# An expert layer's first panels as 512-column products, their two sums added by chains, and a shorter routing

## The chip, the cores and the metric

The kernel runs on one core of one Trainium2 chip. The metric is the time of one execution on the device in microseconds. A row of the profile gives start times from the first instruction of the profiled execution.

## The reference

Two transformer blocks run one behind the other on 256 tokens of width 1024; all is float32. The change lies in `peer`, a layer of 16384 experts that the second block has in each of its two layers (layer 0 and layer 1):

```python
def peer(xn, wq, k1, k2, u_tab, v_tab):
    q = (xt @ wq).reshape(t, PEER_HEADS, D_KEY)          # 8 heads, 2 halves of 128
    s1 = jnp.einsum("thd,hnd->thn", q1, k1)              # 128 keys a half
    s2 = jnp.einsum("thd,hnd->thn", q2, k2)
    v1, i1 = lax.top_k(s1, TOPK)                         # 16 best of each half
    v2, i2 = lax.top_k(s2, TOPK)
    cand = (v1[..., :, None] + v2[..., None, :]).reshape(t, PEER_HEADS, TOPK * TOPK)
    sv, ci = lax.top_k(cand, TOPK)                       # 16 best of the 256 pairs
    e1 = jnp.take_along_axis(i1, ci // TOPK, axis=-1)
    e2 = jnp.take_along_axis(i2, ci % TOPK, axis=-1)
    gates = jax.nn.softmax(sv, axis=-1)
    ...
        hid = jax.nn.gelu(jnp.einsum("td,tkd->tk", xi, u_tab[ei]))
        return jnp.einsum("tk,tkd->td", gi * hid, v_tab[ei])
```

## The kernel before

Every float32 weight panel of 128x1024 is loaded by SyncE (`raw`), copied to a rounded part `whi` by ScalarE (ACT), and the rest `wlo = raw - whi` is made by VectorE (DVE). The tokens stand as two such parts too, `xh` and `xl`, side by side in one tile `xhl`. A product is then three: hi times xh, lo times xh, hi times xl. TensorE (PE) does them at its fast float32 rate. `raw` has four buffers, `whi` and `wlo` three each; `ahead` makes the parts of the panel two further on while a panel is multiplied.

An expert layer does not gather experts: it multiplies all tokens by all of `u` (128 panels of 128 experts), gates the result, and multiplies it by all of `v` (128 panels). It has these stages, here with layer 0's times:

- `wq` (from 1049.0 us): 16 panels make the queries, `scores` the scores, and `firsts` takes the 16 best of each half with `top16` on VectorE: max of eight, their indices, replace, and again.
- `u` (1101.5 to 1529.9 us): 128 panels through `feat`, which does 24 products of 256 columns each: 8 by hi on xh, 8 by lo on xh, 8 by hi on xl. Two panels share one PSUM bank of the pair `w`, and `late` then applies gelu on ACT and multiplies by the gate on DVE.
- beside it on DVE, in this order: what is left of `firsts`, `route(0)` and `route(1)` (the 256 pairs, their 16 best, and the two look-ups by comparing with 0 to 15), and `builds`: for four tokens at a time `onehots` (four `oha` and two `ohb` on DVE, the other two `ohb` on ACT), `gates` (products of these on PE into a PSUM bank, which say how much gate each expert of each token has), and `place`, which moves a bank of gates into `G` and `H`: experts not yet reached are copied by ACT, those already done are multiplied by DVE.
- `v` (from 1531.1 us): 128 panels through `krow`.

The order on each engine is fixed before the run by a planner. `Clock` estimates each instruction, and `Chains` holds the side work as generators. `chains.run()`, called between products, steps a generator when the estimated time of PE has reached its due time: the estimated end of its last step plus 0.2 us less the lead that it yielded (`LEAD_TOP` 1.0, `LEAD_BUILD` 0.8, else 0). `chains.idle()` steps one whether due or not. PSUM has eight banks: two `w`, two `b`, four `acc`. `gates` goes round the four `acc` banks.

The line of nearly all instructions in the trace is that of the helper that records them, L226.

Of the kernel before, what the change touches and what calls it, by code (L numbers as in the profile page):

```python
# [9 lines left out]
F32 = mybir.dt.float32  # L10
# [3 lines left out]
AF = mybir.ActivationFunctionType  # L14
# [274 lines left out]
def net(tc, A, out, stop=None):  # L289
# [3 lines left out]
    with ctx:  # L293
# [86 lines left out]

        banks = [0]

        def feat_sum(dst, other):


            banks[0] += 1
            ps = bank() if banks[0] & 2 else other()
# [10 lines left out]
            chains.run()  # L398
            nc.scalar.activation(dst, ps[:, T:], AF.Copy)
            nc.vector.tensor_tensor(dst, dst, ps[:, :T], op=OP.add)  # L400

        def nat(ps, xh, xl):

# [879 lines left out]
        def peer(l, acc, soon):  # L1283
            with tc.tile_pool(name=f"peer{l}", bufs=1) as p:
# [77 lines left out]
                def route(c):  # L1362
                    r = R[c]
                    v, i, fi, cf, ef, sv, ci, cs, cand = (r[n] for n in ("v", "i", "fi", "cf", "ef", "sv", "ci", "cs", "cand"))
                    nc.vector.tensor_copy(fi, i)
                    for b in (slice(0, 4), slice(4, 8)):
                        nc.vector.tensor_tensor(cand[:, b], v[:, 0, b][:, :, :, None].to_broadcast([128, 4, 16, 16]),
                                                v[:, 1, b][:, :, None, :].to_broadcast([128, 4, 16, 16]), op=OP.add)
                        yield
                    for h in range(8):  # L1370
                        yield from top16(sv[:, h], ci[:, h], cand[:, h].rearrange("p a b -> p (a b)"))
                        yield LEAD_TOP
                    nc.vector.tensor_scalar(cs, ci, 4, None, op0=OP.logical_shift_right)
                    nc.vector.tensor_copy(cf[:, 0], cs)
                    nc.vector.tensor_scalar(cs, ci, 15, None, op0=OP.bitwise_and)
                    nc.vector.tensor_copy(cf[:, 1], cs)
                    yield
                    for s in range(2):
                        for b in (slice(0, 4), slice(4, 8)):
                            nc.vector.tensor_tensor(cand[:, b], cf[:, s, b][:, :, :, None].to_broadcast([128, 4, 16, 16]),  # L1380
                                                    iota[:, None, None, 0:16].to_broadcast([128, 4, 16, 16]),
                                                    op=OP.is_equal)
                            yield
                            nc.vector.tensor_tensor(cand[:, b], cand[:, b],
                                                    fi[:, s, b][:, :, None, :].to_broadcast([128, 4, 16, 16]), op=OP.mult)
                            yield
                            nc.vector.tensor_reduce(ef[:, s, b], cand[:, b], axis=AX.X, op=OP.add)
                            yield
# [20 lines left out]
                state = {"u": 0, "t": 0}  # L1409

                def onehots(t0):
                    a = p.tile([128, 4, 128], F32, name="oha", bufs=2)
# [11 lines left out]

                def gates(t0, a, b):

                    i = t0 // 4 % 4
                    ps = psum.tile([128, 512], F32, name=f"acc{i // 2}{i % 2}", bufs=1)
                    for j in range(4):
                        mm(ps[:, j * 128:(j + 1) * 128], a[:, j], b[:, j], start=True, stop=True)  # L1430
                    return ps
# [23 lines left out]
                        yield LEAD_BUILD  # L1455
                    place(*last)

                def late(e, ps):

                    nt, g = state["t"], rows(e, 2)  # L1460
                    pv = ps.rearrange("p (a t) -> p a t", a=2)
# [237 lines left out]
```

## Time and profile before

| what | before |
|---|---|
| median of 3 runs | 2845.87 us (2844.71 to 2847.70) |
| the profiled execution | 2847.0 us, span 2845.2 us |
| TensorE busy | 2794.8 us, 98% |
| VectorE busy | 2045.7 us, 72% |
| ScalarE busy | 1494.0 us, 53% |
| `u` stage, layer 0 | 1101.5 to 1529.9 us |
| `u` stage, layer 1 | 2060.1 to 2488.4 us |

Durations of neighbours on VectorE and on TensorE overlap in the trace, since an instruction's end is written back while the next one works. What an instruction costs its queue is therefore the distance of two starts, not its duration.

### The profile page before, as it was taken

Reading aid. Unit: us, or ns where it says so; the run is one execution under the profiler, and the core shown is the slowest. Engines: PE = TensorE matmul, PEld = TensorE weight load, DVE = VectorE, ACT = ScalarE, POOL = GpSimd, SP = SyncE. Lnnn points to the kernel's source line nnn. Section 1 sums busy time; section 2 is a strip of 40 time slices with the busy share of each in tenths; the row PEclk is TensorE's granted clock in tenths of the full one; section 3 lists DMA queues with packets and bytes.
Section 4 is the critical chain, followed back from the end, with each engine's and each line's share of the span. In section 5 each row is a group of like instructions: output and inputs, shape, how many; then the busy total and the mean of one; then the engine's idle time right before and its main releaser. Section 6 shows DMA issues by size and latency. Waiting matters only on the chain.

```text
span 2845.2 us, 47840 instructions
## 1 busy us (share of the span) xinstructions
PE 2794.8 (98%) x18786; PEld 2553.3 (90%) x18786; DVE 2045.7 (72%) x3710; ACT 1494.0 (53%) x2423; POOL 100.7 (4%) x104
## 2 busy tenths in 40 slices
PE   9999999999999999999999999999999999999999
PEld 9988889998887889999998888887999999988887
DVE  5556665666766889988995555569898899755555
ACT  4444545544454654447764444456444677544444
POOL 1001010000101100000000000010000000000000
PEclk9999999999999999999999999999999999999999
DMA  6445556544554344554345555543455433455554
GB/s 242 163 164 179 187 176 199 172 148 138 187 192 156 127 144 161 193 181 138 127 138 181 194 195 194 202 159 122 162 180 190 165 127 134 159 190 193 193 194 161
DMA packets 135969, 484.18 MB, mean 170 GB/s; under 512 B 17152, under 2 KB 18176, under 8 KB 135744
## 3 DMA queue, kind: packets, MB, share of 16 engines
q1 hardware_dynamic: 132064, 468.07, 48.2%
q0 software_dynamic: 3680, 13.05, 1.4%
q8 instruction: 148, 2.42, 0.3%
q14 instruction: 77, 0.63, 0.1%
HBM read 479.92 MB, written 1.15 MB: 169 GB/s over the span
## 4 chain that ended last, share of the span: by engine, by line
PE 51%; issue 13%; DVE 2%; ACT 1%; POOL 0%; DVEq 0%; POOLq 0%; ACTq 0%
PE w L226 30%; PE acc L226 19%; DVE G L226 2%; PE b L226 1%; ACT G L226 0%; ACT whi L226 0%; DVE wlo L226 0%; DVE xN L226 0%; ACT ohb L226 0%; POOL r L226 0%; POOL wlo L226 0%; ACT xhl L226 0%; POOL G L226 0%; ACT w L226 0%; DVE nm L226 0%
## 5 line engine op out<-in xcount | busy, mean ns | idle before, releaser
L226 DVE TENSOR_TENSOR wlo<-raw,whi 128x1024 fp32r<-128x1024 f32 (+1 forms) x874 | 1062.6, 1219 | 551.8 <-ACT whi L226 546.1
L226 ACT ACTIVATE whi<-raw 128x1024 fp32r<-128x1024 f32 (+1 forms) x881 | 924.4, 1053 | 673.5 <-PE acc L226 386.4
L226 PE MATMUL w<-xhl,whi 128*128 128x256 f32 (+1 forms) x6176 | 869.5, 292 | 4.4 <-ACT whi L226 4.2
L226 PEld LDWEIGHTS w<-xhl,whi 128*128 128x128 f32 x6176 | 795.4, 193 | 20.8 <-ACT whi L226 5.0
L226 PE MATMUL acc<-whi,xhl 128*128 128x512 f32 x2048 | 550.2, 390 | 2.4 <-ACT xhl L226 2.4
L226 PE MATMUL w<-xhl,wlo 128*128 128x256 f32 x3248 | 462.4, 286 | 9.4 <-DVE wlo L226 9.3
L226 PEld LDWEIGHTS acc<-whi,xhl 128*128 128x128 f32 x2048 | 384.5, 188 | 82.3 <-ACT xhl L226 2.8
L226 PEld LDWEIGHTS w<-xhl,wlo 128*128 128x128 f32 x3248 | 422.5, 193 | 15.4 <-DVE wlo L226 11.2
L226 PE MATMUL acc<-wlo,xhl 128*128 128x512 f32 x1024 | 317.7, 389 | 0.0
L226 PEld LDWEIGHTS acc<-wlo,xhl 128*128 128x128 f32 x1024 | 192.3, 188 | 39.8
L226 ACT ACTIVATE G<-w 128x512 f32<-128x512 f32 (+16 forms) x157 | 81.6, 520 | 203.1 <-PE w L226 202.6
L226 DVE TENSOR_SCALAR oha<-iota,e1T,gT 128x128 f32<-128x128 f32 x512 | 152.8, 341 | 0.0
L226 PE MATMUL acc<-ohb,oha 128*128 128x128 f32 x1024 | 136.7, 276 | 0.3
L226 PEld LDWEIGHTS acc<-ohb,oha 128*128 128x128 f32 x1024 | 125.9, 192 | 2.0 <-ACT ohb L226 1.4
L226 PE MATMUL w<-whi,xhl 128*128 128x256 f32 x640 | 121.2, 287 | 0.0
L226 PEld LDWEIGHTS w<-whi,xhl 128*128 128x128 f32 x640 | 101.9, 193 | 2.3 <-issue 2.1
L226 PE MATMUL w<-wlo,xhl 128*128 128x256 f32 x320 | 91.3, 285 | 0.3
L226 POOL TENSOR_TENSOR r<-v,minus_half 128x1 f32<-128x1 f32 x26 | 21.8, 840 | 1959.5 <-DVE v L226 1959.5
L226 ACT ACTIVATE ohb<-iota,me2T 128x128 f32<-128x128 f32 x256 | 87.5, 392 | 0.7 <-PE acc L226 0.7
L226 PE MATMUL b<-xhl,whi 128*128 128x512 f32 x320 | 80.2, 393 | 0.0
L226 DVE TENSOR_TENSOR xhl<-G,xhl 128x512 fp32r<-128x512 f32 x112 | 76.5, 684 | 0.0
L226 DVE TENSOR_TENSOR G<-G,acc 128x272 f32<-128x272 f32 (+22 forms) x128 | 66.5, 520 | 8.5 <-ACT H L226 8.2
(303 smaller groups left out, 2962.1 us busy)
## 6 DMA issues: line engine op xcount, KB each, us to landing
raw<-u SPq DMA_DIRECT2D x256, 512.0 KB, 3.2
raw<-v SPq DMA_DIRECT2D x256, 512.0 KB, 3.3
raw<-ffn SPq DMA_DIRECT2D x132, 512.0 KB, 4.0
raw<-mix SPq DMA_DIRECT2D x90, 512.0 KB, 3.3
raw<-att SPq DMA_DIRECT2D x80, 512.0 KB, 3.3
raw<-ret SPq DMA_DIRECT2D x63, 512.0 KB, 3.3
bias<-scr POOLq DMA_DIRECT2D x12, 512.0 KB, 7.1
G<-norm_g SPq DMA_DIRECT2D x4, 512.0 KB, 5.6
```

The lines of the kernel that those rows point to most:

```text
L226: return f(*args, **kw)
```

## The change

`feat_both` does a `u` panel as `feat_sum` did elsewhere already: 8 products by hi on both parts of the tokens (512 columns), 8 by lo on xh (256 columns). The sum of hi times xl lands in the second half of a whole PSUM bank, the rest in the first half. For each panel a new chain `value` copies the second half to SBUF on ACT and adds the first half on DVE. Behind each second panel comes `late` on the SBUF tile `u`. `u` lies in `xN`, whose content (the residual) is written to DRAM ahead of the stage and read back behind it.

A panel now takes one bank, of the pair `w` or of `acc10`, `acc11`; so `gates` alternates between the two banks `acc00` and `acc01`. A panel is not begun while the sum three back is still to be handed out.

Only pairs whose two ranks are small enough can be among the 16 best of the 256; `RANKS` lays them out in 64 places. `top16` runs over these 64, some small operations turn a place into its two ranks, and the look-ups of ranks 8 to 15 compare with 16 values, those of ranks 0 to 7 with 8. `LEAD_TOP` becomes 2.0 and most steps of `route` yield `LEAD_ROUTE` 2.0.

```diff
-LEAD_TOP = 1.0
+LEAD_TOP = 2.0
+LEAD_ROUTE = 2.0
+RANKS = ((0, 0, 1, 16), (16, 1, 1, 8), (24, 2, 2, 8), (40, 4, 4, 4), (56, 8, 8, 1))
...
+        def feat_both(ps):
             hi, lo = W.get()
             for k in range(8):
                 mm(ps, hi[:, k * 128:(k + 1) * 128], xhl[:, :, k], start=k == 0, stop=False)
...
                 mm(ps[:, :T], lo[:, k * 128:(k + 1) * 128], xh[:, k], start=False, stop=k == 7)
             W.ahead("lo")
             chains.run()
...
+                kept = dram.tile([128, 2, D], F32, name=f"kept{l}")
+                nc.gpsimd.dma_start(kept, xN)
...
-                    for b in (slice(0, 4), slice(4, 8)):
-                        nc.vector.tensor_tensor(cand[:, b], v[:, 0, b][:, :, :, None].to_broadcast([128, 4, 16, 16]),
-                                                v[:, 1, b][:, :, None, :].to_broadcast([128, 4, 16, 16]), op=OP.add)
-                        yield
+                    few = flat[:, :512].rearrange("p (h n) -> p h n", h=8)
+                    for o, a0, na, nb in RANKS:
...
                     for h in range(8):
-                        yield from top16(sv[:, h], ci[:, h], cand[:, h].rearrange("p a b -> p (a b)"))
+                        yield from top16(sv[:, h], ci[:, h], few[:, h])
                         yield LEAD_TOP
...
                     for s in range(2):
-                        for b in (slice(0, 4), slice(4, 8)):
...
+                        for k0, nr in ((0, 8), (8, 16)):
+                            q = flat[:, :64 * nr].rearrange("p (h k a) -> p h k a", h=8, k=8)
...
                 def gates(t0, a, b):
 
-                    i = t0 // 4 % 4
-                    ps = psum.tile([128, 512], F32, name=f"acc{i // 2}{i % 2}", bufs=1)
+                    ps = aux(t0 // 4 % 2)
...
+                def value(e, j, u, ps):
+                    nc.scalar.activation(u[:, j], ps[:, T:], AF.Copy)
+                    yield
+                    nc.vector.tensor_tensor(u[:, j], u[:, j], ps[:, :T], op=OP.add)
+                    state["b"] += 1
+                    if j:
+                        yield
+                        late(e, u)
+
+                hid = xN.rearrange("p c (i a t) -> p (c i) a t", i=2, a=2)
                 for e in range(0, 128, 2):
-                    ps = bank()
+                    if e == 80:
+                        while state["t"] == 0:
+                            chains.idle()
+                    u = hid[:, e // 2 % 4]
                     for j in range(2):
-                        if e == 80 and j == 0:
-                            while state["t"] == 0:
-                                chains.idle()
-                        feat(ps[:, j * T:(j + 1) * T], xh, xl)
-                    late(e, ps)
+                        n = e + j
+                        while n - state["b"] > 3:
+                            chains.idle()
+                        ps = bank() if n & 2 else psum.tile([128, 512], F32, name=f"acc1{n % 2}", bufs=1)
+                        feat_both(ps)
+                        chains.add(value(e, j, u, ps), "value", 0)
                 chains.drain()
+                nc.gpsimd.dma_start(xN, kept)
```

The order of TensorE differs in the two `u` stages alone. There `builds` began behind panel 68 and its last `gates` came behind panel 114, 64 of them over 47 panels; now it begins behind panel 57 and the last comes behind panel 92, 64 over 35 panels. TensorE's order in the middle of `builds`, layer 0, before (`w` with `xhl` is a `u` panel, `acc` with `ohb` a `gates`):

```order
L226 MATMUL acc_14317<-ohb,oha 128x128 x4
L226 MATMUL w<-xhl,whi 128x256 x8
L226 MATMUL w<-xhl,wlo 128x256 x8
L226 MATMUL acc_14358<-ohb,oha 128x128 x4
L226 MATMUL w<-xhl,whi 128x256 x16
L226 MATMUL w<-xhl,wlo 128x256 x8
L226 MATMUL acc_14411<-ohb,oha 128x128 x4
```

The same place of TensorE's order after:

```order
L228 MATMUL acc_13143<-ohb,oha 128x128 x4
L228 MATMUL w<-xhl,wlo 128x256 x8
L228 MATMUL acc_13177<-ohb,oha 128x128 x4
L228 MATMUL w<-xhl,whi 128x512 x8
L228 MATMUL acc_13209<-ohb,oha 128x128 x4
L228 MATMUL w<-xhl,wlo 128x256 x8
L228 MATMUL acc_13240<-ohb,oha 128x128 x4
L228 MATMUL acc_13259<-xhl,whi 128x512 x8
```

A `gates` now stands behind every half panel, two a panel, where 64 over 47 panels were 1.4.

VectorE's order in the same place before (`G<-G,acc` is the multiplication of a `place`, `G<-G,w` that of `late`):

```order
L226 TENSOR_TENSOR wlo<-raw,whi 128x1024
L226 TENSOR_SCALAR oha<-iota,e1T,gT 128x128 x3
L226 TENSOR_SCALAR ohb<-miota,me2T 128x128
L226 TENSOR_SCALAR oha<-iota,e1T,gT 128x128
L226 TENSOR_SCALAR ohb<-miota,me2T 128x128
L226 TENSOR_TENSOR G<-G,acc_13862 128x78x4
L226 TENSOR_TENSOR G<-G,w 128x2x76
L226 TENSOR_TENSOR wlo<-raw,whi 128x1024
```

And after (`xN<-xN,acc` and `xN<-xN,w` are the added sums, `G<-G,xN` is `late`):

```order
L228 TENSOR_TENSOR G<-G,acc_13080 128x64x4
L228 TENSOR_TENSOR xN<-xN,acc_13067 128x256
L228 TENSOR_SCALAR oha<-iota,e1T,gT 128x128 x3
L228 TENSOR_SCALAR ohb<-miota,me2T 128x128
L228 TENSOR_SCALAR oha<-iota,e1T,gT 128x128
L228 TENSOR_SCALAR ohb<-miota,me2T 128x128
L228 TENSOR_TENSOR G<-G,acc_13111 128x64x4
L228 TENSOR_TENSOR G<-G,xN 128x2x76
L228 TENSOR_TENSOR wlo<-raw,whi 128x1024
```

Two builds now carry one `wlo`, one added sum and, in every second panel, one `late`; before, a `wlo` stood behind 1.4 builds and there were no added sums.

## Rows read from the trace of the kernel before

**Rows 1.** The page, part 1: busy time, share of the span, instructions.

```profile
PE 2794.8 (98%) x18786; PEld 2553.3 (90%) x18786; DVE 2045.7 (72%) x3710; ACT 1494.0 (53%) x2423; POOL 100.7 (4%) x104
```

**Rows 2.** Windows: stretch, length, busy us of each engine, PEclk, DMA share, GB/s.

```profile
1101.50:1298.00 196.50, 196.50 (x1641) 196.50 (x1640) 173.71 (x365) 96.80 (x113) 0.00 (x0) 1.00 0.53 183
1298.00:1490.00 192.00, 191.85 (x1629) 190.99 (x1629) 181.67 (x516) 142.90 (x406) 0.00 (x0) 1.00 0.38 133
1490.00:1530.00 40.00, 39.94 (x334) 39.73 (x332) 22.75 (x25) 17.42 (x23) 0.00 (x0) 1.00 0.50 171
...
2060.00:2488.00 428.00, 427.86 (x3598) 427.00 (x3598) 378.08 (x904) 257.15 (x539) 0.00 (x0) 1.00 0.47 159
```

**Rows 3.** Timeline of PE, two `u` panels: start us, us, instruction and count.

```profile
1112.02 1.12 PE L226 MATMUL w<-xhl,wlo 128*128 128x256 f32 x8
...
1114.90 1.12 PE L226 MATMUL w<-xhl,wlo 128*128 128x256 f32 x8
```

**Rows 4.** Timeline of PE, two panels that `feat_sum` did elsewhere.

```profile
231.10 2.00 PE L226 MATMUL b<-xhl,whi 128*128 128x512 f32 x8
...
233.89 2.00 PE L226 MATMUL w<-xhl,whi 128*128 128x512 f32 x8
```

**Rows 5.** Timeline of DVE inside `builds`.

```profile
1404.98 1.22 DVE L226 TENSOR_TENSOR wlo<-raw,whi 128x1024 fp32r<-128x1024 f32 x1
1406.11 0.86 DVE L226 TENSOR_SCALAR oha<-iota,e1T,gT 128x128 f32<-128x128 f32 x3
...
1407.53 0.54 DVE L226 TENSOR_TENSOR G<-G,acc 128x368 f32<-128x368 f32 x1
1407.98 1.23 DVE L226 TENSOR_TENSOR wlo<-raw,whi 128x1024 fp32r<-128x1024 f32 x1
```

**Rows 6.** Timeline of PE inside `builds`.

```profile
1404.08 1.12 PE L226 MATMUL w<-xhl,whi 128*128 128x256 f32 x8
1405.04 1.06 PE L226 MATMUL acc<-ohb,oha 128*128 128x128 f32 x8
...
1406.88 1.12 PE L226 MATMUL w<-xhl,wlo 128*128 128x256 f32 x8
```

**Rows 7.** Waits of DVE from 1298 to 1490 us: total, times, longest.

```profile
DVE wlo L226 <- ACT whi L226: 4.3, 11, 0.5
DVE G L226 <- ACT H L226: 2.8, 8, 0.5
DVE G L226 <- ACT w L226: 2.7, 7, 0.5
```

**Rows 8.** Timeline of DVE: starts of a `top16`, and of what follows it.

```profile
1118.39 0.28 DVE L226 MAX8 G<-G 128x8 f32<-128x128 f32 x1
...
1120.11 0.28 DVE L226 MAX8 G<-G 128x8 f32<-128x128 f32 x1
...
1158.89 0.42 DVE L226 MAX8 G<-G 128x8 f32<-128x256 f32 x1
...
1161.28 1.20 DVE L226 TENSOR_TENSOR wlo<-raw,whi 128x1024 fp32r<-128x1024 f32 x1
```

**Rows 9.** Groups by form, DVE, 1101.5 to 1530 us: a look-up's comparison.

```profile
L226 DVE TENSOR_TENSOR H<-H,iota 128x1024 f32<-128x1024 f32 x4 | 4.9, 1219 | 0.0
```

**Rows 10.** Timeline of DVE: the `wlo` for the lo part that starts at 1114.90.

```profile
1112.82 1.22 DVE L226 TENSOR_TENSOR wlo<-raw,whi 128x1024 fp32r<-128x1024 f32 x1
```

**Rows 11.** Timeline from the last `u` panel to the first `v` panel.

```profile
1529.97 0.58 ACT L226 ACTIVATE w<-w 128x512 f32<-128x512 f32 x1 [1.82 <-PE w L226]
1530.47 1.14 ACT L226 ACTIVATE xhl<-G 128x512 fp32r<-128x512 f32 x2
1531.14 0.73 PE L226 MATMUL acc<-whi,xhl 128*128 128x512 f32 x2 [1.21 <-ACT xhl L226]
```

**Rows 12.** Groups by form, whole span: the copy and the sum that follow `feat_sum`.

```profile
L226 ACT ACTIVATE up<-w 128x256 f32<-128x256 f32 x20 | 7.7, 384 | 27.7 <-PE w L226 27.7
L226 DVE TENSOR_TENSOR up<-up,w 128x256 f32<-128x256 f32 x20 | 8.4, 421 | 11.7 <-ACT up L226 11.7
```

More of the change, by code (lines that the diff above doesn't have):

```diff
@@ L381, in net @@
         banks = [0]
-        def feat_sum(dst, other):
-            banks[0] += 1
-            ps = bank() if banks[0] & 2 else other()
+        def feat_both(ps):
             hi, lo = W.get()
@@ L398, in feat_sum @@
             chains.run()
+        def feat_sum(dst, other):
+            banks[0] += 1
+            ps = bank() if banks[0] & 2 else other()
+            feat_both(ps)
             nc.scalar.activation(dst, ps[:, T:], AF.Copy)
             nc.vector.tensor_tensor(dst, dst, ps[:, :T], op=OP.add)
+            chains.run()
         def nat(ps, xh, xl):
@@ L1365, in route @@
                     nc.vector.tensor_copy(fi, i)
-                    for b in (slice(0, 4), slice(4, 8)):
-                        nc.vector.tensor_tensor(cand[:, b], v[:, 0, b][:, :, :, None].to_broadcast([128, 4, 16, 16]),
-                                                v[:, 1, b][:, :, None, :].to_broadcast([128, 4, 16, 16]), op=OP.add)
-                        yield
+                    flat = cand.rearrange("p h a b -> p (h a b)")
+                    few = flat[:, :512].rearrange("p (h n) -> p h n", h=8)
@@ L1370, in route @@
+                    for o, a0, na, nb in RANKS:
+                        sh = [128, 8, na, nb]
+                        nc.vector.tensor_tensor(few[:, :, o:o + na * nb].rearrange("p h (a b) -> p h a b", a=na),
+                                                v[:, 0, :, a0:a0 + na, None].to_broadcast(sh),
+                                                v[:, 1, :, None, 0:nb].to_broadcast(sh), op=OP.add)
+                    yield LEAD_ROUTE
                     for h in range(8):
-                        yield from top16(sv[:, h], ci[:, h], cand[:, h].rearrange("p a b -> p (a b)"))
+                        yield from top16(sv[:, h], ci[:, h], few[:, h])
@@ L1372, in route @@
                         yield LEAD_TOP
[L1373 to L1377, printed above, removed]
-                    for s in range(2):
-                        for b in (slice(0, 4), slice(4, 8)):
[L1380 to L1388, printed above, removed]
+                    t0, t1, t2 = (flat[:, j * 128:(j + 1) * 128].rearrange("p (h k) -> p h k", h=8) for j in range(3))
@@ new lines, in route @@
+                    ra, rb = cf[:, 0], cf[:, 1]
+                    nc.vector.tensor_copy(t0, ci)
+                    for t, n in ((t1, 3), (t2, 2)):
+                        nc.vector.tensor_scalar(cs, ci, n, None, op0=OP.logical_shift_right)
+                        nc.vector.tensor_copy(t, cs)
+                    yield LEAD_ROUTE
+                    nc.vector.tensor_scalar(t1, t1, -1.0, 0.0, op0=OP.add, op1=OP.max)
+                    nc.vector.scalar_tensor_tensor(t1, t2, -6.0, t1, op0=OP.add, op1=OP.max)
@@ new lines, in route @@
+                    nc.vector.scalar_tensor_tensor(ra, t0, -48.0, t1, op0=OP.add, op1=OP.max)
+                    yield LEAD_ROUTE
+                    nc.vector.tensor_scalar(t1, ra, 8.0, 8.0, op0=OP.mult, op1=OP.add)
+                    nc.vector.scalar_tensor_tensor(t1, ra, 16.0, t1, op0=OP.mult, op1=OP.min)
+                    nc.vector.tensor_scalar(t2, ra, 4.0, 24.0, op0=OP.mult, op1=OP.add)
+                    nc.vector.scalar_tensor_tensor(t2, ra, 48.0, t2, op0=OP.add, op1=OP.min)
+                    nc.vector.tensor_tensor(t1, t1, t2, op=OP.min)
@@ new lines, in route @@
+                    nc.vector.tensor_tensor(rb, t0, t1, op=OP.subtract)
+                    yield LEAD_ROUTE
+                    for s in range(2):
+                        for k0, nr in ((0, 8), (8, 16)):
+                            q = flat[:, :64 * nr].rearrange("p (h k a) -> p h k a", h=8, k=8)
+                            sh, ks = [128, 8, 8, nr], slice(k0, k0 + 8)
+                            nc.vector.tensor_tensor(q, cf[:, s, :, ks, None].to_broadcast(sh),
+                                                    iota[:, None, None, 0:nr].to_broadcast(sh), op=OP.is_equal)
+                            yield LEAD_ROUTE
+                            nc.vector.tensor_tensor(q, q, fi[:, s, :, None, 0:nr].to_broadcast(sh), op=OP.mult)
+                            yield LEAD_ROUTE
+                            nc.vector.tensor_reduce(ef[:, s, :, ks], q, axis=AX.X, op=OP.add)
+                            yield LEAD_ROUTE
@@ L1407, in route @@
                     yield
-                state = {"u": 0, "t": 0}
+                state = {"u": 0, "t": 0, "b": 0}
                 def onehots(t0):
@@ L1456, in builds, with late @@
                     place(*last)
-                def late(e, ps):
+                def late(e, pv):
                     nt, g = state["t"], rows(e, 2)
-                    pv = ps.rearrange("p (a t) -> p a t", a=2)
                     if nt < T:
@@ L1470, in peer @@
                     chains.add(work, 1, 1)
+                def value(e, j, u, ps):
[7 more added lines that the diff above has]
+                hid = xN.rearrange("p c (i a t) -> p (c i) a t", i=2, a=2)
                 for e in range(0, 128, 2):
-                    ps = bank()
+                    if e == 80:
+                        while state["t"] == 0:
+                            chains.idle()
+                    u = hid[:, e // 2 % 4]
                     for j in range(2):
-                        if e == 80 and j == 0:
-                            while state["t"] == 0:
-                                chains.idle()
-                        feat(ps[:, j * T:(j + 1) * T], xh, xl)
-                    late(e, ps)
+                        n = e + j
+                        while n - state["b"] > 3:
+                            chains.idle()
+                        ps = bank() if n & 2 else psum.tile([128, 512], F32, name=f"acc1{n % 2}", bufs=1)
+                        feat_both(ps)
+                        chains.add(value(e, j, u, ps), "value", 0)
                 chains.drain()
+                nc.gpsimd.dma_start(xN, kept)
                 acc = acc_banks()
```

## Prediction

> **What bounds the kernel now.** I read the page first: TensorE is busy 98% of the span and VectorE 72% [rows 1]. Such shares average over stages, so next I cut layer 0's `u` stage into windows. In all of it TensorE is busy to within 0.2 us, and its granted clock is 1.00, the 2.4 GHz level [rows 2]. So the stage lasts as long as its products take. VectorE follows closely: 173.7 of 196.5 us (88%) beside the routing, 181.7 of 192.0 us (95%) beside `builds`, and 57% only in the last 40 us [rows 2]. Layer 1's stage is the same one again, with 378.1 of 428.0 us [rows 2]. So a change in this stage has two limits to keep in view: what TensorE saves, and whether VectorE still fits.
>
> All else in the program keeps its order on every engine (some `wlo` of the `wq` stage change places with pieces of `top16`), so the sum is made per `u` stage and doubled.
>
> **The products.** A panel by 24 products of 256 columns takes 2.88 us, from one lo part's start to the next's [rows 3]. The new form runs elsewhere already: there a panel takes 233.89 - 231.10 = 2.79 us [rows 4]. The column count is the same, 6144, but there are 8 fewer instructions. I take 0.087 us a panel, the unrounded difference being 0.08 to 0.10: 128 panels save 11.1 us a stage (bounds 10 and 13). It counts in full only where TensorE does not wait.
>
> The Trainium skill, page "TensorE: Matmul & The Clock Gate", section "Back-to-back issue gap", gives N/2.4 + 2.5 ns for N columns: an estimate by it is 2.62 us for the old panel and 2.60 us for the new. By that the change would save 0.02 us a panel instead of 0.09. The rows show both forms at a larger price, and their own difference is used.
>
> **VectorE beside `builds`.** This is the term that decides. First the prices, as distances of starts [rows 5]: a `wlo` 1.13 us (1404.98 to 1406.11), the six one-hot operations of a build 1.42 us (to 1407.53), a `place` multiplication of 368 columns 0.45 us. The line through 368 and 1024 columns is 0.07 us plus 1 ns for each 0.96 columns, so 256 columns take 0.34 us. An added sum of 256 columns is such an operation too; its full duration is 0.42 us [rows 12], and 0.34 us is what it costs in a queue. As a test, the stage before holds 46 `wlo`, 64 builds, 62 `place` of 354 columns on average and 23 `late` of 275: 52 + 91 + 27 + 8 = 178 us, where the trace has 181.7 us busy [rows 2].
>
> After the change the order has, between the first and the last `gates` of a stage, 34 `wlo`, 64 builds, 37 added sums, 62 `place` of 286 columns on average (fewer experts are done so early) and 18 `late` of 256: 38.4 + 90.9 + 12.6 + 22.9 + 6.1 = 170.9 us, less the first build's 1.42 us, which stands ahead of the first `gates`: 169.5 us.
>
> TensorE in the same stretch has 35 panels at 2.79 us and 63 `gates`. A `gates` costs 1406.88 - 1404.08 less 16 products at 0.12 us, so 0.88 us [rows 6]. That is 97.7 + 55.4 = 153.1 us. VectorE is 16.4 us short.
>
> Can TensorE run ahead of it? Before, `gates` went round four banks, and a build was handed out when VectorE was nearly done, so TensorE never waited long and panels filled the time: 47 panels to 64 builds. Now two banks alternate. A `gates` waits until the `place` two builds back has emptied its bank, and that `place` is the newest thing on VectorE's queue. So TensorE and VectorE go in step, and behind the waiting `gates` stand the products of the next half panel. The planner sees its own TensorE wait, finds the next build due at each half panel, and hands out two a panel. The excess cannot be put off either: `gates` 63 needs `place` 61. I take 15.5 us of wait a stage, the shortfall less about 1 us by which VectorE may be ahead at the start. Bounds: 11 us if the prices are 3% too high, and 25 us if all of VectorE's own waits for ACT in that stage, 4.3 + 2.8 + 2.7 us [rows 7], remain on top. They come from ACT having a bank or a `whi` not ready; with VectorE the later one most of them should go.
>
> The Trainium skill, page "Perfetto Trace Analysis", section "Optimizing Tensor Performance", says that independent products should rotate through different PSUM banks so that emptying one overlaps the next group. It speaks against going from four banks to two, but gives no price.
>
> **VectorE beside the routing.** There are now 57 panels, 159 us of TensorE. A `top16` over 128 values takes 1.72 us and one over 256 takes 2.39 us [rows 8]; on the line through both, one over 64 takes 1.38 us. So 16 of them save 16 us. Of 24 look-up operations at 1.22 us [rows 9] 12 are halved: 6 us. The pairs' sums save 3 us, some 20 small operations of 0.2 us add 4 us, 54 added sums 18 us. VectorE's total: 57 x 1.13 + 54 x 0.34 + (173.7 - 68 x 1.13) - 16 - 6 - 3 + 4 = 64 + 18 + 97 - 21 = 158 us against 159. It just fits as a mean, not everywhere. The first 12 panels each carry a `wlo`, an added sum and a `top16` of 128 left from `firsts`: 1.13 + 0.34 + 1.72 = 3.19 us against 2.79, 4.8 us over. The cushion is small: a `wlo` that ended at 1114.04 was needed at 1114.90, 0.86 us later [rows 3, 10], and the lo part now starts some 0.9 us later in its panel, since 8 products of 512 columns stand ahead of it instead of 8 of 256. 4.8 - 1.7 gives 3 us of wait a stage (bounds 0 and 8, since the rest of the stretch runs at 99%). The longer leads let VectorE's queue be filled earlier; they make no work less.
>
> **The end of the stage.** Now gelu starts at 1529.97, and the first `v` product at 1531.14 waits for the split of its rows behind it on ACT [rows 11]. After the change a copy (0.38 us) and an added sum (0.42 us) [rows 12] stand ahead of gelu, and signals between: 0.9 us more a stage (0.5 to 1.5).
>
> **At no cost.** The residual's way to DRAM and back is two copies of 1 MB on POOL's queue. The first has the whole `wq` stage (52 us) before `value` writes there; the second has the `v` stage (some 350 us) before the residual is read. Nothing on POOL is due in either time, and DMA is half idle (0.38 to 0.53 [rows 2]). Without that cover a copy would cost its transfer once. ACT gets 128 copies more but is 50 to 75% busy [rows 2].
>
> **Sum.** A stage: -11.1 + 15.5 + 3.0 + 0.9 = +8.3 us; two: +16.6 us. The profiled execution took 2847.0 us (span 2845.2 and 1.8 around it), which is 1.1 us over the median of 2845.87. So 2847.0 + 16.6 - 1.1 = 2862.5, say **2863 us**.
>
> **Rivals.**
> 1. *VectorE keeps up* (the other side: faster). The mechanism is the same queue. Per two panels and four builds it would have to take no more than TensorE's 5.58 + 3.52 = 9.1 us. By the rows it takes 2.26 (two `wlo`) + 0.68 (two sums) + 5.68 (four builds) + 1.48 (four `place`) + 0.3 (one `late`) = 10.4. Were it under 9.1, only the saving and the end would be left: 2 x (-11.1 + 0.9) = -20, 2826 us. For it: the stage as a whole has room, some 395 us of VectorE against 413 of TensorE. Against it: the order is fixed and puts the builds together. 7%.
> 2. *Half of it*: no wait beside the routing, and 9 to 11 us beside `builds`, with the full 13 us saved. 2 x (-13 + 10 + 0.9) = -4, around 2842 to 2850 us. 12%.
> 3. *ACT's waits stay on top*: VectorE idles for banks that ACT empties, and 25 us are lost a stage: 2 x (-11.1 + 25 + 3 + 0.9) = +36, 2882 us and up to 2892. 13%.
> 4. *The new panel is no shorter here* (the change doesn't do what it says). 512-column products might run slower beside this stage's traffic, 0.02 us a panel saved: 2 x (-2.6 + 19.4) = +34, 2880 us; the page's formula above would say so. The rows of `feat_sum` speak against it. 4%.
>
> **How the numbers follow.** The forecast has 64%, with 2850 to 2880 as its own range from the bounds. The range that is to hold the time 8 times in 10 takes in most of case 2 and the lower half of cases 3 and 4: 2846 to 2886. Faster or slower by over 0.2% (5.7 us, about what a measurement here can tell from no change) starts at 2840.2 and 2851.6 us: faster is case 1 and a little of case 2, 8%; the same is the rest of case 2 and the forecast's lower edge, 13%; slower 79%.
>
> **What would show it.** In the `u` windows TensorE should no longer be busy throughout: waits in front of `gates` for DVE, of 0.2 to 0.5 us each, some 15 us a stage, and VectorE busy 97% or more there. A panel without `gates` should take 2.79 us. `wlo` waits of TensorE in the first dozen panels should add up to 3 us. The gap ahead of `v` should be near 2.1 us instead of 1.2. I am wrong if TensorE is busy beside `builds`, which would mean that VectorE's prices in a queue are lower than the starts show, or if the waits name ACT.

## The result

The changed kernel takes **2870.25 us** (median of 4 runs, 2867.31 to 2874.66), the kernel before, measured beside it, 2845.93 us (4 runs, 2844.71 to 2847.7). The ratio is 1.0086, with a 95% interval of 1.0069 to 1.0104. The change makes the kernel 24 us slower; the forecast was 17 us slower, 2863 us.

The page of the profiled execution after (2874.66 us), part 1, with engine, busy us, share and instructions, answers to [rows 1]:

```profile
span 2872.9 us, 44542 instructions
PE 2807.3 (98%) x16738; PEld 2447.9 (85%) x16738; DVE 2087.8 (73%) x4028; ACT 1576.7 (55%) x2677; POOL 100.0 (3%) x108
```

TensorE's share is what it was: the page alone shows nothing of the loss. The windows do. Layer 0's `u` stage after, cut at the first and behind the last `gates`, and the first 4.5 us of the `v` stage (stretch, length, busy us of PE, PEld, DVE, ACT and POOL, granted clock, DMA share, GB/s); they answer to [rows 2]:

```profile
1098.30:1266.00 167.70, 163.31 (x929) 141.73 (x927) 157.03 (x437) 98.73 (x155) 0.00 (x0) 1.00 0.60 183
1266.00:1437.30 171.30, 168.05 (x1075) 143.36 (x1076) 171.30 (x537) 140.87 (x422) 0.00 (x0) 1.00 0.36 108
1437.30:1537.40 100.10, 100.03 (x574) 87.88 (x572) 70.36 (x91) 58.81 (x90) 0.00 (x0) 1.00 0.60 187
1539.44:1543.94 4.50, 4.50 (x13) 3.56 (x14) 2.58 (x4) 1.42 (x2) 0.53 (x1) 0.62 0.78 264
```

Beside the routing TensorE is idle for 4.4 us. Beside `builds` VectorE is busy for all of the 171.3 us and TensorE is not; the 3.3 us that it shows as idle there are far less than its wait, as the timeline below shows. Behind the last `gates` TensorE is busy throughout again. In the fourth row the granted clock is 0.62, which nothing in the prediction spoke of.

From the first `u` product to the first `v` product the stage takes 441.1 us in both layers, before 429.6: 2 x 11.5 = 23.0 of the 24.3 us between the medians. The profiled execution is the longest of the four; 1.6 us of it are in layer 0's `v` stage (the fourth row). Between layer 0's last and layer 1's first expert stage, a stretch with the same products in both kernels, it took 187 us against 181, at a mean granted clock of 0.95 against 1.00; in the other runs, of either kind, that stretch varies from 180.8 to 187.1 us.

**Beside `builds`.** The timeline of PE after (start, us, instruction, count; in brackets the idle time ahead and what ended it):

```profile
1339.99 1.13 PE L228 MATMUL acc<-ohb,oha 128*128 128x128 f32 x8 [0.25 <-DVE G L228]
1340.88 1.19 PE L228 MATMUL w<-xhl,wlo 128*128 128x256 f32 x8
1342.09 1.13 PE L228 MATMUL acc<-ohb,oha 128*128 128x128 f32 x8
1342.98 2.09 PE L228 MATMUL acc<-xhl,whi 128*128 128x512 f32 x8
1345.00 1.13 PE L228 MATMUL acc<-ohb,oha 128*128 128x128 f32 x8
```

One panel and two builds from 1339.99 to 1345.00: 5.01 us. By the prices of the prediction TensorE has 2.79 + 2 x 0.88 = 4.55 us of work in it. The same panel on DVE:

```profile
1340.10 0.84 DVE L228 TENSOR_SCALAR oha<-iota,e1T,gT 128x128 f32<-128x128 f32 x3
...
1341.52 0.43 DVE L228 TENSOR_TENSOR G<-G,acc 128x280 f32<-128x280 f32 x1
1341.88 1.21 DVE L228 TENSOR_TENSOR wlo<-raw,whi 128x1024 fp32r<-128x1024 f32 x1
1343.01 0.84 DVE L228 TENSOR_SCALAR oha<-iota,e1T,gT 128x128 f32<-128x128 f32 x3
...
1344.43 0.43 DVE L228 TENSOR_TENSOR G<-G,acc 128x280 f32<-128x280 f32 x1
1344.79 0.40 DVE L228 TENSOR_TENSOR xN<-xN,w 128x256 f32<-128x256 f32 x1
1345.12 0.84 DVE L228 TENSOR_SCALAR oha<-iota,e1T,gT 128x128 f32<-128x128 f32 x3
```

Two builds at 1.42, two `place` at 0.36, a `wlo` at 1.13 and an added sum at 0.33 are 5.02 us, with no gap between any two. So the panel lasts as long as VectorE's queue. The waits of PE and of PEld (the weight loads, which go ahead of the products) from 1266 to 1437 us:

```profile
PE acc L228 <- DVE G L228: 1.8, 7, 0.3
PE acc L228 <- ACT xN L228: 0.4, 1, 0.4
```

```profile
PEld acc L228 <- issue: 14.3, 38, 0.7
```

Only 1.8 us are put down to VectorE. The rest shows as PEld's "issue" ahead of `acc`, as it seems because the load of a `gates`' operand goes first, and the trace shows no releaser for it. The size of the wait is therefore read from the stretch: 170.5 us from the first to the last `gates` (1265.97 to 1436.5). Less the 153.1 us of TensorE's work that the prediction's prices give, 17.4 us are left. That is too much, because a `gates` costs more than those prices say: in e3 below TensorE is busy throughout a stretch of 68 panels and 63 `gates` that takes 247.8 us, and (247.8 - 68 x 2.79) / 63 is 0.92 us, not 0.88. By that price the work is 35 x 2.79 + 63 x 0.92 = 155.6 us and the wait **14.9 us**. DVE has no wait at all in this stretch.

**Beside the routing**, waits of PE from 1098.3 to 1266 us, and one place of the timeline (DVE, then PE):

```profile
PE w L228 <- DVE xN L228: 2.3, 3, 1.4
PE acc L228 <- DVE G L228: 0.9, 1, 0.9
PE w L228 <- DVE wlo L228: 0.5, 1, 0.5
```

```profile
1114.80 1.22 DVE L228 TENSOR_TENSOR wlo<-raw,whi 128x1024 fp32r<-128x1024 f32 x1
1115.93 0.29 DVE L228 MAX8 G<-G 128x8 f32<-128x128 f32 x1
...
1117.51 0.41 DVE L228 TENSOR_TENSOR xN<-xN,w 128x256 f32<-128x256 f32 x1
```

```profile
1116.26 1.10 PE L228 MATMUL acc<-xhl,wlo 128*128 128x256 f32 x8
1118.07 2.08 PE L228 MATMUL w<-xhl,whi 128*128 128x512 f32 x8 [0.71 <-DVE xN L228]
```

The largest wait by total is not for a `wlo`. In the place shown a panel cannot start because its bank still holds the sum of four panels back (that is the one which `n - state["b"] > 3` waits for, not the sum three back), and the added half of that sum stands on VectorE's queue behind a `top16` (1115.93 to 1117.51).

**The end of the stage**, timeline of all engines, answers to [rows 11]:

```profile
1537.37 0.38 ACT L228 ACTIVATE xN<-w 128x256 f32<-128x256 f32 x1 [1.45 <-PE w L228]
1537.79 0.42 DVE L228 TENSOR_TENSOR xN<-xN,w 128x256 f32<-128x256 f32 x1 [0.61 <-ACT xN L228]
1538.24 0.63 ACT L228 ACTIVATE xN<-xN 128x512 f32<-128x512 f32 x1 [0.48 <-DVE xN L228]
1538.78 1.13 ACT L228 ACTIVATE xhl<-G 128x512 fp32r<-128x512 f32 x2
1539.44 1.09 PE L228 MATMUL acc<-whi,xhl 128*128 128x512 f32 x2 [2.11 <-ACT xhl L228]
```

A copy, an added sum and a gelu in a row now, and the gap ahead of the first `v` product is 2.11 us where it was 1.21.

### The profile page after: what moved, and what is told of

Read it like the earlier page. It is cut to its first block, busy times and chain, and to the rows that moved or that the text cites. A ratio compares the mean times of both kernels' runs of the same rounds, so it can differ in the third digit from the quotient of the medians.

```text
span 2872.9 us, 44542 instructions
## 1 busy us (share of the span) xinstructions
PE 2807.3 (98%) x16738; PEld 2447.9 (85%) x16738; DVE 2087.8 (73%) x4028; ACT 1576.7 (55%) x2677; POOL 100.0 (3%) x108
## 5 line engine op out<-in xcount | busy, mean ns | idle before, releaser
L228 PE MATMUL w<-xhl,whi 128*128 128x256 f32 (+1 forms) x3104 | 586.3, 335 | 7.9 <-DVE xN L228 4.6
L228 PEld LDWEIGHTS w<-xhl,whi 128*128 128x128 f32 x3104 | 469.0, 192 | 58.4 <-issue 7.5
L228 PE MATMUL w<-xhl,wlo 128*128 128x256 f32 x2224 | 317.4, 286 | 8.7 <-DVE wlo L228 8.6
L228 PEld LDWEIGHTS w<-xhl,wlo 128*128 128x128 f32 x2224 | 296.1, 192 | 24.3 <-DVE wlo L228 12.5
L228 PE MATMUL acc<-xhl,whi 128*128 128x512 f32 (+1 forms) x1088 | 269.7, 389 | 2.5 <-DVE G L228 1.8
L228 PEld LDWEIGHTS acc<-xhl,whi 128*128 128x128 f32 x1088 | 191.6, 189 | 36.2 <-issue 2.6
L228 PE MATMUL acc<-ohb,oha 128*128 128x128 f32 x1024 | 144.1, 283 | 7.3 <-DVE G L228 3.7
L228 PE MATMUL acc<-xhl,wlo 128*128 128x256 f32 x1056 | 149.8, 285 | 0.0
L228 PEld LDWEIGHTS acc<-xhl,wlo 128*128 128x128 f32 x1056 | 141.5, 190 | 8.6 <-DVE wlo L228 0.8
L228 ACT ACTIVATE G<-xN 128x512 f32<-128x512 f32 (+18 forms) x110 | 61.7, 561 | 129.2 <-DVE xN L228 128.2
```

The costliest lines, as they stand in the source:

```text
L228: return f(*args, **kw)
```

## Experiments

The theory: beside `builds` TensorE waits because two builds a panel give VectorE more work than TensorE has, and two banks keep the engines in step; the leads and the end of the stage add the rest. The main rivals: each `gates` pays for the hand-over of its bank, whatever VectorE has to do, or VectorE has too much work in the whole stage. "Stage" is the time from the first `u` product to the first `v` product, in both layers alike to 0.4 us; the ratio is to the kernel before as measured beside each run (2846 to 2847 us).

| run | us | ratio, 95% | stage, us |
|---|---|---|---|
| before | 2845.9 | 1 | 429.6 |
| changed | 2870.3 | 1.0086 (1.0069 to 1.0104) | 441.1 |
| e1, four banks | 2841.5 | 0.9982 (0.9973 to 0.9992) | 426.2 |
| e2, before with two banks | 2898.6 | 1.0188 (1.0171 to 1.0205) | 454.9 |
| e3, builds held back | 2840.0 | 0.9978 (0.9969 to 0.9988) | 426.2 |
| e4, leads back | 2861.9 | 1.0048 (1.0032 to 1.0065) | 435.7 |
| e5, e3 and e4 | 2827.6 | 0.9930 (0.9916 to 0.9943) | 421.2 |
| e6, e1 and e4 | 2829.5 | 0.9939 (0.9925 to 0.9952) | 421.2 |
| e7, e2 held back | 2847.8 | 1.0002 (0.9992 to 1.0011) | 429.0 |
| e8, before with the new routing | 2857.7 | 1.0033 (1.0021 to 1.0045) | 435.0, 435.4 |
| e9, changed with the old routing | 2853.0 | 1.0023 (1.0013 to 1.0032) | 433.6 |
| e10, e8 with the leads back | 2852.0 | 1.0020 (1.0011 to 1.0030) | 432.5 |
| e11, no added sum | 2852.4 | 1.0016 (1.0006 to 1.0026) | 433.0 |
| e12, e6 with the old last pair | 2827.2 | 0.9931 (0.9918 to 0.9945) | 420.4 |

### e1: four banks for `gates` in the changed kernel

```diff
-                    ps = aux(t0 // 4 % 2)
+                    i = t0 // 4 % 4
+                    ps = psum.tile([128, 512], F32, name=("acc00", "acc01", "b0", "b1")[i], bufs=1)
```

> The changed kernel with one thing undone: `gates` goes round four PSUM banks again (acc00, acc01, b0, b1). Theory (builds and panels in step through two banks, VectorE 100% busy): the order now spreads the 64 builds over 61 panels instead of 35, VectorE needs some 3.5 us a panel against 3.7 us of TensorE, so the 16 us of wait a stage shrink to 0 to 2. A stage is then -11.1 (products) + 5.5 (waits beside the routing) + 1 + 0.9 (end) = -3.7 us: 2839 us, 2834 to 2844. Rival (VectorE has too much work in the stage whatever the banks): 2866 to 2874 us, VectorE still near 100% between the first and last gates.

Measured 2841.5 us: the theory's. The planner now spreads the 64 builds over 61 panels in place of 35, and beside them PE has one wait of 0.4 us, for ACT. A stage gains 14.9 us. But two things changed together, the banks and the pace of the builds. e3 and e7 part them.

### e2: two banks in the kernel before

```diff
-                    i = t0 // 4 % 4
-                    ps = psum.tile([128, 512], F32, name=f"acc{i // 2}{i % 2}", bufs=1)
+                    ps = aux(t0 // 4 % 2)
```

> The kernel before with one part of the change alone: `gates` alternates between two banks. Theory: its order puts 64 builds beside 31 panels instead of 47; VectorE needs 31 x 1.13 + 90.9 + 26 + 5 - 1.4 = 156 us there, TensorE 31 x 2.88 + 55.4 = 145 us, so 11 us of wait a stage: 2868 us, 2860 to 2874. Rival (two banks hold no one up, the added sums do): 2844 to 2848 us.

Measured 2898.6 us: the direction is the theory's, but the size, 25 us a stage, is over twice the 11 us that it gave, and the time lies above its range. Window and DVE's waits between the first and the last `gates`:

```profile
1297.74:1471.02 173.28, 159.33 (x1263) 150.66 (x1264) 160.32 (x492) 123.43 (x376) 0.00 (x0) 1.00 0.31 100
```

```profile
DVE G L226 <- ACT H L226: 11.0, 30, 0.7
```

The kernel before does 46.7 panels and 63 `gates` in 192.2 us without a wait of TensorE, so a `gates` costs 0.92 us here too, and TensorE has 31.3 panels x 2.88 + 63 x 0.92 = 148.1 us of work in these 173.3. Of the 25.2 us of wait, VectorE's 160.3 us of work explain 12, about the 11 that I had counted; its waits for ACT are 11 more. How they come about, in one place (ACT, then DVE, then PE):

```profile
1364.31 0.44 ACT L226 ACTIVATE G<-w 128x320 f32<-128x320 f32 x1 [1.46 <-PE w L226]
...
1365.01 1.05 ACT L226 ACTIVATE whi<-raw 128x1024 fp32r<-128x1024 f32 x1
...
1367.15 0.21 ACT L226 ACTIVATE H<-acc 128x64 f32<-128x64 f32 x1
```

```profile
1367.40 0.49 DVE L226 TENSOR_TENSOR G<-G,acc 128x320 f32<-128x320 f32 x1 [0.49 <-ACT H L226]
```

```profile
1368.04 1.13 PE L226 MATMUL acc<-ohb,oha 128*128 128x128 f32 x8 [0.82 <-DVE G L226]
```

ACT waits 1.46 us for the end of a pair of panels to do its gelu; behind that stand a `whi`, one-hot operations and the copy that empties a `gates` bank; the `place` on VectorE waits for that copy, and the next `gates` for the `place`. Three in-order engines wait for one another in a ring, which two banks are too few to break at this pace. This is the mechanism of my third rival. It does not occur in the changed kernel, where DVE waits for nothing beside `builds`.

### e3: two banks, builds held back

```diff
-LEAD_BUILD = 0.8
+LEAD_BUILD = -0.6
```

> The changed kernel with its two banks kept and LEAD_BUILD at -0.6 instead of 0.8, so that a build is handed out 1.4 us later by the planner: 64 builds over 68 panels, one a panel. Theory (the pace of the builds against VectorE's queue costs the time): TensorE's waits beside builds fall to 0 to 2 us a stage, 2839 us, 2834 to 2846. Rival (each of the 64 gates pays some 0.25 us for its bank, since the place two builds back is always recent): 14 to 17 us a stage stay, 2866 to 2874 us.

Measured 2840.0 us: the theory's, and the rival's price of a hand-over is out. With the two banks of the changed kernel, but one build a panel, TensorE is busy in every us between the first and the last `gates`:

```profile
1265.50:1513.30 247.80, 247.80 (x1600) 224.07 (x1600) 234.48 (x626) 189.04 (x510) 0.00 (x0) 1.00 0.48 144
```

### e4: the leads back

```diff
-LEAD_TOP = 2.0
-LEAD_ROUTE = 2.0
+LEAD_TOP = 1.0
+LEAD_ROUTE = 0.0
```

> The changed kernel with LEAD_TOP at 1.0 and LEAD_ROUTE at 0, as far as the leads of before go. Theory for the waits beside the routing (6 us a stage: the leads fill VectorE's queue with up to 2 us of top16 and look-ups ahead of a wlo or an added sum): they fall to 0 to 2 us a stage, the waits beside builds stay: -9 us in all, 2861 us, 2857 to 2865. Rival (the load itself, 3.2 us of VectorE a panel against 2.79 in the first dozen panels): no change, 2867 to 2873 us.

Measured 2861.9 us: the leads cause most of the waits beside the routing. The same window (from the first `u` product to the first `gates`) and PE's waits in it:

```profile
1098.77:1269.20 170.43, 169.29 (x969) 147.63 (x967) 162.47 (x447) 103.09 (x161) 0.00 (x0) 1.00 0.63 189
```

```profile
PE acc L228 <- ACT ohb L228: 0.7, 1, 0.7
PE acc L228 <- DVE wlo L228: 0.2, 1, 0.2
PE w L228 <- DVE wlo L228: 0.2, 1, 0.2
```

VectorE is as full in it (162.5 of 170.4 us), and yet TensorE is idle for 1.1 us instead of 4.4. The window holds 59.5 panels, the changed kernel's 57, so 7.0 us of products more in 2.7 us more: 4.3 of the 5.4 us by which the stage is shorter. The rest lies in the stretch of builds, which has half a panel more in about the same time (170.7 us). So most of the waits came from the order in VectorE's queue, not from the amount of its work.

### e5 and e6: both cures together

e5 is e3's and e4's edit in one kernel, e6 is e1's and e4's.

> The changed kernel with its two banks for gates, LEAD_BUILD from 0.8 to -0.6, LEAD_TOP back to 1.0 and LEAD_ROUTE to 0.0. The order now has 64 builds between panels 59.5 and 127.5, one a panel, and pieces of the routing without the longer leads. Theory: the two waits are separate and add up. Holding the builds back took 2870 to 2840 (15 us a stage), the shorter leads took 2870 to 2862 and took the waits beside the routing (some 5.5 us a stage by the u stage's length, 441.1 to 435.7). Together: 2840 - 2 x 5.5 = 2829 us, range 2825 to 2834. Rival: VectorE simply has too much to do in the whole stage, and a wait removed in one place comes back in the other: 2838 to 2842.

> The changed kernel with gates round four banks (acc00, acc01, b0, b1) and both leads back (LEAD_TOP 1.0, LEAD_ROUTE 0.0); LEAD_BUILD stays 0.8. The order spreads the 64 builds over panels 59.5 to 121.5. Theory as before, from the run with four banks alone (2841.5) less 2 x 5.5 us: 2830 us, range 2826 to 2835. Rival: a wait removed in one place comes back in the other: 2839 to 2843.

Measured 2827.6 and 2829.5 us, both inside the theory's ranges, and both faster than either kernel of this case. The stage is 421.2 us in both: 14.9 + 5.4 of the changed kernel's 441.1 would leave 420.8. The two waits add up, and nothing comes back elsewhere.

### e7: two banks in the kernel before, builds held back

The edits of e2 and e3 together, on the kernel before.

> The kernel before with gates on two banks, as in the run that took 2898.6 us, and in addition LEAD_BUILD at -0.6. The order spreads the 64 builds over panels 68 to 126.7, one a panel, in place of 68 to 99. Theory: two banks cost nothing by themselves; what cost 26 us a stage there was the pace of two builds a panel, at which VectorE has 158 us of work and 11 more of waits for banks that ACT empties against 146 us of TensorE. At one a panel TensorE has 2.88 + 0.88 = 3.76 us and VectorE some 3.4, so: 2846 us, range 2843 to 2853. Rival: in this kernel ACT's waits (a gelu or a whi for the panel's end, with the copies of a place behind it) go with the two banks at any pace and keep half of the loss: 2865 to 2890.

Measured 2847.8 us, no difference from before: the theory's. At one build a panel the ring of e2 does not close either:

```profile
1296.20:1522.30 226.10, 226.09 (x1919) 225.82 (x1920) 201.84 (x546) 157.64 (x416) 0.00 (x0) 1.00 0.43 139
```

VectorE still waits for ACT here (12.0 us for a `whi`, 8.7 for a gelu's bank, 2.5 for `H`), but TensorE never does: the waits fall into VectorE's slack.

### e8, e9 and e10: the parts alone

e8 is the kernel before with the routing's part of the diff and its leads. e9 is the changed kernel with the old routing and `LEAD_TOP` 1.0. e10 is e8 with e4's edit.

> The kernel before with the new routing alone (candidates by RANKS, top16 over 64, halved look-ups, LEAD_TOP and LEAD_ROUTE 2.0); the products of 256 columns, the four banks and the end of the stage as before. The order has the builds from panel 48.3 to 89.7. Theory (longer leads make wlo late when VectorE is close to full): VectorE is at some 91% beside the routing without the added sums, so TensorE waits 1 to 4 us a stage there, and some 0 to 3 us beside the builds: 2850 us, range 2846 to 2857. Rival (the added sums are what fills VectorE; leads alone do no harm): no wait, 2843 to 2847. Second rival (less work of VectorE is a gain of its own): below 2840, which would need TensorE to wait for VectorE in the kernel before.

> The changed kernel with the old routing (256 candidates, top16 over 256, whole look-ups, LEAD_TOP 1.0 and no lead elsewhere); new products, added sums, gates on two banks. The order has the 64 builds from panel 79.25 to 122.25: 43 of them two a panel, the rest one a panel. Theory (only builds at two a panel wait): 43 of 64 builds at the wait of 17.4 us per 64 give 11.7 us a stage; -12 us for the products, +0.9 at the end, 0 to 3 beside the routing, where VectorE would have some 213 of 223 us: 2 x 2 over 2846, 2850 us, range 2842 to 2858. Rival (new routing is what costs, two banks nothing): 2824 to 2832. Second rival (VectorE too full beside the old routing, more than 5 us a stage): above 2858.

> As the run with the new routing alone (2857.7 us), with LEAD_TOP back to 1.0 and LEAD_ROUTE to 0.0. The order has the builds from panel 54.3 to 96.3. In the run with the leads TensorE waited 4 us beside the routing (two lo parts 0.9 us each, 1.9 us at the first gates) and 2 us beside the builds, a stage. Theory (the leads put pieces of the routing ahead of a wlo): the waits beside the routing go, 2846 to 2851 us, 2848. Rival (less work of VectorE lets the builds come earlier and in a denser bunch, whatever the leads): 2854 to 2859.

e8 took 2857.7 us, by its ratio 9 us over before, and 0.7 us above the upper end of the theory's range; less work alone is no gain, since TensorE waited for nothing before. e9 took 2853.0 us, inside the theory's range: its stretch of builds is 189.8 us against 43 x 2.79 + 63 x 0.88 = 175.4 of TensorE, 14.4 us of wait by the prediction's prices and 11.9 with 0.92 us a `gates` (11.7 expected), and VectorE is busy for all of it. Alone the parts cost 5.6 and 4.0 us a stage, together 11.5, so each brings most of its own loss.

e10 took 2852.0 us, between its theory (2846 to 2851) and its rival (2854 to 2859). The leads are half of the routing's cost; 2.9 us a stage remain without them, of which 1.7 us are one wait of the first `gates` for an `ohb` of ACT. Where the rest goes was not traced further. Part of that half may be the clock's: behind the same 1.7 us wait the granted clock averages 0.67 and 0.68 over 4.5 us in the two layers of e8, and 1.00 in both of e10.

### e11: no added sum

```diff
-                    nc.vector.tensor_tensor(u[:, j], u[:, j], ps[:, :T], op=OP.add)
```

> The changed kernel without VectorE's added sum in value(): the first part of each sum is left out of the result, all else stays; the order keeps the builds at two a panel (panels 48.5 to 79.5). Theory (the wait beside the builds is VectorE's total less TensorE's): VectorE has 31 x 1.13 + 89.5 + 22.9 + 6 = 153.4 us, TensorE 31 x 2.79 + 55.4 = 141.9, so 11.5 us of wait in place of 17.4, and beside the routing no more than 1 us: a stage of -12 + 11.5 + 1 + 0.5 = +1 us, 2848 us, range 2842 to 2854. Rival (the wait belongs to each gates, a hand-over of the bank of 0.27 us whatever VectorE has to do): 17.4 us again, and 2858 to 2864.

Measured 2852.4 us, the theory's, and 6 us under the rival. The stretch of builds takes 152.9 us, where VectorE's sum gave 153.4 and a wait as long as the changed kernel's would give 159.3. By the prediction's prices the wait is 11.0 us (11.5 expected, 17.4 in the changed kernel), with 0.92 us a `gates` it is 8.5 (14.9). The builds are as dense and the banks as few as there, and the wait shrinks with VectorE's work, which still fills its time (149.96 us busy, 2 us of waits):

```profile
1241.05:1393.95 152.90, 151.67 (x1008) 133.65 (x1008) 149.96 (x483) 135.05 (x407) 0.00 (x0) 0.99 0.37 108
```

### e12: the last pair in the old form

```diff
+                    if e == 126:
+                        ps = bank()
+                        for j in range(2):
+                            feat(ps[:, j * T:(j + 1) * T], xh, xl)
+                        while state["u"] < 126:
+                            chains.idle()
+                        late(e, ps.rearrange("p (a t) -> p a t", a=2))
+                        break
                     for j in range(2):
```

> The kernel of the run with four banks and the leads back (2829.5 us), and in addition the last two panels of the u stage in the old form: 24 products of 256 columns each into the halves of one bank, gelu right behind them, no copy and no added sum. In every run with the new end the first v product waits 2.1 us for the split, the granted clock is then at 0.61 to 0.66 over the next 4.5 us, and the v stage behind it is 1.6 us longer (349.7 in place of 348.1); with the kernel before's gap of 1.2 us, and in the run without the added sums, neither is there. Theory (the longer gap costs its length and a stretch at the low level of the clock): the gap is 1.2 us again, the clock stays at 1.00, a v stage takes 348.1 us; less 0.9 and 1.6, plus 0.2 for two panels: 2 x 2.3, 2825 us, range 2822 to 2828. Rival (the clock falls there for another reason, such as the new stage's pattern of products): only the gap comes back, 2828 us, and 0.6 stays in the windows.

Measured 2827.2 us, in the theory's range, but only 2 us under e6, which was measured at another time, and the runs can't tell that from none. The rows can. The gap ahead of `v` is as short as before, the stage 0.8 us shorter than e6's, and the granted clock behind it is 1.00 in both layers:

```profile
1520.68:1525.18 4.50, 4.50 (x20) 3.73 (x21) 2.86 (x5) 2.81 (x4) 0.00 (x0) 1.00 0.70 258
```

One sentence of the expectation is wrong: the clock does not fall behind the longer gap "in every run". The sentence rested on layer 0 of a few profiles. Over both layers of the seven profiles with the 2.1 us gap (the changed kernel, e1, e3, e4, e5, e6, e9) it falls in 9 of 14 cases. In the other seven profiles (before, e2, e7, e8, e10, e12, and e11, whose gap is half a us shorter) it falls in none of 14. Where it falls, the `v` stage takes 349.7 us, elsewhere 348.1. In e6's own profile only layer 1 pays for it, so the gain to expect from the clock was 1.6 us, not 3.2. e12 also changes the products ahead of the gap, so by itself it does not part the gap from their pattern. e8 does: all its `u` products are of the old form, and its clock falls behind the 1.7 us wait in both layers.

## Why the prediction was right, point by point

**The bound.** Right: the stage lasts as long as TensorE's products and its waits, and VectorE is the engine that it waits for.

**The products, -11.1 us a stage.** Right. Away from the builds, starts of two panels after:

```profile
1500.86 2.00 PE L228 MATMUL w<-xhl,whi 128*128 128x512 f32 x8
...
1503.66 2.00 PE L228 MATMUL acc<-xhl,whi 128*128 128x512 f32 x8
```

2.80 us. Most of the saving is seen where the waits are gone: e12, with 126 of 128 panels in the new form and the old end, has a stage 9.2 us under that of before, where 126 x 0.087 = 11.0 would be all of it. Of the other 1.8 us, 1.1 are waits of TensorE that are left in e12's stage (0.7 for an `ohb`, 0.4 for two `wlo`); the rest was not traced. By the formula of the Trainium skill, page "TensorE: Matmul & The Clock Gate", section "Back-to-back issue gap", the panel would be an estimated 2.60 us. The section gives that formula for a product by itself, which the prediction left out, and says that in a stream with weight loads it counts too much at 512 columns. Here it counts too little: the trace has 2.80 us, and the measurement decides.

**Beside `builds`, +15.5 us.** Right in mechanism and in size: 14.9, which is also what e1 and e3 win back. VectorE's sum was 170.9 us and the window has 171.3, all busy. That the size is so near is in part luck, since errors cancel: the stretch between the outer `gates` takes 170.5 us where VectorE's sum gave 169.5, the 1 us that I took off for a head start of VectorE is not seen, and TensorE's work was priced 2.5 us too low (153.1 for 155.6). e3 and e11 show that it is VectorE's work against TensorE's, and not the banks' hand-over. The Trainium skill, page "Perfetto Trace Analysis", section "Optimizing Tensor Performance", has independent products rotate through different banks. e1 agrees, at 14.9 us a stage; e3 and e7 add what the rule leaves open: at a pace that the emptying engine can keep, two banks cost nothing.

**Beside the routing, +3.0 us.** This is the step that failed, in its reason and in its size: the leads alone cost 5.4 us by e4, inside the bounds of 0 to 8. I put it down to the amount of work of the first 12 panels and costed the longer leads at nothing ("they make no work less"). The amount was right, 158 us for VectorE where the window has 157.0 busy. e4 keeps the work, takes the leads away, and most of the waits go. A lead of 2 puts pieces of the routing on VectorE's queue ahead of a `wlo` and ahead of an added sum; the added sum holds a bank, which the prediction's working did not count as a path.

**The end, +0.9 us.** Right for the gap (2.11 against 1.21). What it set off, the low clock and 1.6 us more of the `v` stage in 9 of 14 cases, was not foreseen.

**At no cost.** Right, as far as the stages show. Where the granted clock stays at 1.00, the `v` stage, beside which the residual comes back, takes 348.1 us in the changed kernel as before. The stretch ahead of layer 1's `u` stage, in which it goes out, takes 180.8 to 180.9 us in e3, e5 and e12, which have the copies, and 180.8 before.

**The sum.** Predicted +8.3 us a stage, measured +11.5. The runs give its parts: 14.9 us beside `builds` (e1, e3), 5.4 for the leads (e4), and -8.4 for the products, the end and what waits are left when both cures are in (e5, 421.2 against 429.6), where the products and the end alone were put at -10.2. That makes +11.9, 0.4 us over the stage. So the forecast was short by 2.4 us for the leads and 1.8 for a smaller net saving, and over by 0.6 beside `builds`. Twice 11.5, and 1.6 us for each of the `v` stages that start at the low clock, are 23 to 26 us, where the medians differ by 24.3.

**The rivals.** VectorE did not keep up (1), and the loss was not half (2). ACT's waits did not stay on top here (3), but e2 shows that they do, at 11 us a stage, in the kernel before with two banks. The new panel is as short as elsewhere (4). The sentence that the excess "cannot be put off" held only for the order as written: at `LEAD_BUILD` -0.6 the planner puts it off at no cost.

## What to carry to other kernels

Compare two engines in the stretch where a loop couples them, at the pace at which the work is handed out there: the stage as a whole had room on VectorE, and the kernel lost 15 us a stage because builds came two a panel. When buffers are cut, slow the pace of what fills them (here one constant, with the leads undone, turned 24 us of loss into 20 of gain). And a lead that lets one engine's optional work be queued early is not free, since what is needed next, a part of the weights or a sum that holds a bank, then stands behind it.

## What the runs showed of the hardware

A wait that is hidden in the weight loads is nearly invisible in the list of waits: of 14.9 us of TensorE's wait beside `builds`, 1.8 us appear under VectorE's name, and PEld's list has 14.3 us as "issue". TensorE's busy time hides it too: 168.05 of 171.30 us.

A pause of TensorE ahead of the `v` stage cost more than its length when it grew from 1.2 to 2.1 us: in 9 of 14 cases the granted clock then averages 0.62 to 0.67 over the next 4.5 us, a time at 1.2 GHz and not 2.4, and 1.6 us are lost. With the pause at 1.2 us that was seen in none of 12 cases, nor in the two of e11 with 1.65 us. The same stands ahead of the first `gates` in the `u` stage: a pause of 2.2 us was followed by 0.62 in both layers of e11, one of 1.7 us by 0.67 and 0.68 in e8, but by 1.00 in both layers of e10. So the length of the pause alone does not decide, and what does the runs don't show.
